# Tying weight splits behind copies, and one pass for bias and maximum, in a two-layer attention kernel

## The chip, the cores and the metric

One core of one Trainium2 chip runs the whole program. The metric is device time in microseconds, the median of three runs: 751.36 us before the change (750.59 to 751.94). A profile of one execution stands beside it, with the start and end of each instruction on each engine: TensorE (PE in the profile, PEld for its weight loads), VectorE (DVE), ScalarE (ACT), GpSimd (POOL) and SyncE (SP, which issues nearly all DMAs).

## The reference

Two layers on 256 positions of width 1024, 16 heads of 64. Layer 0 mixes three dilated windows of attention with rotary positions, layer 1 is a forgetting attention; each is followed by a SwiGLU block of width 2816, and a last RMS norm ends the program. All arrays are float32. The part of layer 1 that the change touches:

```
s = jnp.einsum('bihd,bjhd->bhij', qi, k).astype(jnp.float32) * scale
s = s + ci[..., None] - ck[:, :, None, :]
s = jnp.where(key_pos[None, :] <= qpos[:, None], s, NEG_INF)
p = jax.nn.softmax(s, axis=-1)
return jnp.einsum('bhij,bjhd->bihd', p, vf)
```

Here `c` is the running sum of the log forget gates. In layer 0 the queries and keys get `partial_rotary` first, a product with cosines plus a permuted product with sines.

## The kernel before, in words

**Split products.** TensorE multiplies in a reduced form of fp32. To keep precision each float32 operand is split into a high half (`wh` for weights; ACT copies the raw tile, L74) and a low half (`wl`; DVE subtracts the high half from the raw tile, L78), and each product is three matmuls (`mm3`, L197 and L202): high by high, high by low, low by high. So each weight tile that arrives costs ACT and DVE an instruction for each 1024 columns; `split` issues them.

**The stream of weights.** `order` lists all weight pieces in the order in which they are used. `weights(name, i)` loads and splits everything up to two pieces ahead (`AHEAD = 2`) and returns the piece wanted. A piece comes as two DMAs of 512 KB into `raw` (five buffers), and each is split into `wh` and `wl` (four buffers each). A raw buffer is free again when the low half has read it. The program is written in one stream; a scheduler orders each engine's instructions by what is written first, except that `first()` moves an instruction up to 300 places ahead, and `issue_after(x)` holds one back until x has been issued. Each engine then works strictly in its order.

**Layer 0.** The projections run unit by unit (one of queries, keys or values of one group for a quarter of the heads, 48 matmuls of 256 columns for a query or key unit). `rotated` turns a query or key unit: a shuffle (L433), a product with the cosines straight from PSUM (`read`, L434), a product with the sines (L435) and an addition (L436). A projection's PSUM tile (`mm`, two buffers) is free again after L433 and L434. For the first unit, `rcos` and `rsin` are first multiplied by the rows' norm factors (L569).

**Layer 1.** Heads go in four quarters of four heads; a quarter is a query unit, a key unit and, for the last quarter, a value unit. `proj_feat` gives queries or keys in PSUM, and ACT copies them to `fb` (L939). After the first half of the next unit PE computes the scores of the quarter's first pair of heads (`scores_b`, L855), and after its second half those of the second pair. For each pair of heads:

- DVE adds the bias, 384 columns for each head, from PSUM and `bias` to `p` (L861);
- DVE takes the negated maximum of 128 and of 256 columns (L865), two query blocks of each head;
- ACT takes the exponential with that maximum as bias and sums the row (`exps`, L283);
- DVE takes the reciprocal of the sums (L870), and ACT (L872) and DVE (L873) scale.

Then `trans_b` transposes the four heads' probabilities on PE (L293, from `p` to PSUM), copies them to `pt` (L297), and `pv_b` multiplies with the values (L304) and splits the result (`oth`, `otl`). The `bias` tile comes by a DMA issued on SP from a buffer in memory, and POOL adds the causal mask to two of its blocks (L841). Low halves of two weight calls are kept in the list `behind` and issued after the gates' scan or after the last bias addition (`release`).

Of the kernel before, what the change touches and what calls it, by code (L numbers as in the profile page):

```python
# [12 lines left out]
AF = mybir.ActivationFunctionType  # L13
# [18 lines left out]
def trunk(ctx: ExitStack, tc: tile.TileContext, T, out):  # L32
# [10 lines left out]
    def first():  # L43

        return tc.high_priority(offset=300)
# [22 lines left out]
    euler = cst.tile([P, 1], F32, name="euler")  # L68
    nc.gpsimd.memset(euler, math.e)

    def split(pair, view, src, early=True, after=None):
        hi, lo = pair
        with first() if early else nullcontext():
            a = nc.scalar.activation(view(hi), src, AF.Copy)  # L74

            def low(after=None):
                with tc.issue_after(after.ins) if after else nullcontext():
                    return nc.vector.tensor_tensor(view(lo), src, view(hi).bitcast(F32), op=ALU.subtract)  # L78

            if isinstance(after, list):  # L80
                return after.append(low)
            return a, low(after)


    def piece(key, todo=None):
        if key[0][:2] == "dn" and key[1] == LATE:
            wh, wl = (y.rearrange("p k c -> p (k c)") for y in fm_tile("ot", KT, 1))
        else:
            wh, wl = (wp.tile([P, WIDE], F32R, tag=y, name=y, bufs=4) for y in ("wh", "wl"))
        if key == GATED:  # L90
            wh, wl = (y.rearrange("p (k c) -> p k c", k=KT) for y in (wh, wl))
        for c in range(2):
            raw = wp.tile([P, 1024], F32, tag="raw", name="raw", bufs=5)
            u = slice(c * 1024, (c + 1) * 1024)
            nc.sync.dma_start(raw, T[key[0]][key[1]][:, u])
            view = lambda y, u=u: y[:, u]
            if key == GATED:
                raw = raw.rearrange("p (k c) -> p k c", c=256)
                view = lambda y, c=c: y[:, c * 4:c * 4 + 4, :256]
            cut = lambda after=None, raw=raw, view=view: split((wh, wl), view, raw, False, after)  # L100
            if todo is None:
                cut()
            else:
                todo.append(cut)
        if key == GATED:
            cut = lambda after=None: split((wh, wl), lambda y: y[:, :, 256:], wf32, False, after)
            todo.append(cut)
        return wh, wl

# [35 lines left out]
    ready = {}  # L145
    state = {"next": 0}

    def weights(nm, i, after=None, ahead=AHEAD):

        upto = order.index((nm, i)) + ahead  # L150
        while state["next"] <= min(upto, len(order) - 1):
            key = order[state["next"]]
            cuts = []
            ready[key] = piece(key, cuts)
            for cut in cuts:
                cut(after)
            state["next"] += 1
        return ready.pop((nm, i))

# [365 lines left out]
    def later(i, fn, *a):  # L525
        due.setdefault(i, []).append((fn, a))

    quads = [{"hq": hq, "fm": {}, "pt": {}, "v": {}} for hq in range(4)]
    for i, (hq, g, w) in enumerate(a_units):
        quad = quads[hq]  # L530
        if i == 3:
            o = o_next
        elif i:

            wt = weights("a_in", hq * 9 + g * 3 + w, read if i > 4 else None)
        if i != 3 and (w < 2 or g == 0 and hq > 1):
            o = psum("mm")
        if i == 1:
            ident = const("ident", [P, P])
            rcos = const("rcos", [P, S])  # L540
            rsin = const("rsin", [P, S])
        if i == 2:
            mask0 = const("mask0", [P, 3 * P])
            mask12 = const("mask12", [P, S])
        if i in (24, 31):
            x.append(hrow("x"))
            t = len(x) - 1
            nc.sync.dma_start(x[t], T["x"][t * P:(t + 1) * P, :])
        if w < 2:
            for c in range(2):  # L550
                if i == 3 and c == 0:
                    continue
                proj_feat(xt, wt, o[:, c * S:(c + 1) * S], c, (KT // 2, rstd_a) if i == 2 and c == 1 else None)
            if i == 2:
                values_12(quad["v"], lead)

                wt = weights("a_in", 1)
                o_next = psum("mm")
                rb = psum("tr")

                def rows():
                    for t in range(2):
                        nc.tensor.matmul(rb[:, t * P:(t + 1) * P], r_a[t].to_broadcast([P, P]), ident,
                                         start=True, stop=True)

                proj_feat(xt, wt, o_next[:, :S], 0, (6, rows))
                with first():
                    for c in (rcos, rsin):
                        nc.vector.tensor_tensor(c, c, rb[:, :S], op=ALU.mult)  # L569
            q, read = rotated(o, g, w)  # L570
            quad["fm"][g, w] = q
            if w == 1:

                j = i + (hq == 0)
                if g == 0:
                    for pr in range(2):
                        later(j + 2 + pr, scores_a, quad, g, pr)
                else:
                    later(j + 3 - g, scores_a, quad, g)
                if g == 2:  # L580
                    later(j + 1, softmax_a, quad)
                    j = 9 * hq + 11 + 2 * (hq == 0)
                    for pr in range(2):
                        later(j + pr, trans_a, quad, pr)
                        later(j + 1 + pr, pv_a, quad, pr)
        elif g == 0 and hq > 1:
            for t in range(2):
                proj_tok(xt, wt, o[:, t * S:(t + 1) * S], t)
            quad["v"][0] = v_tile(o, r_a)
        elif i > 1:  # L590


            half = hq % 2 if g == 0 else g - 1
            if half == 0:

                lead = [psum("mm" if g else "o") for _ in range(2)]
            proj_pair(xt, wt, lead, half)
            if half and g == 0:
                vs = [v_tile() for _ in range(2)]
                for t in range(2):  # L600
                    v_pair(vs, lead[t], t, r_a[t])
                for y in range(2):
                    quads[hq - 1 + y]["v"][0] = vs[y]
            elif half:
                values_12(quad["v"], lead)
        for fn, a in due.pop(i, ()):
            fn(*a)
# [239 lines left out]
    def scores_b(hq, pr):  # L847
        b = bq[hq]
        nm = stat_tile("nm_b", 4)
        den = stat_tile("den_b", 4)  # L850
        pt = b.setdefault("pt", {})
        scs = [psum("sc") for _ in range(2)]
        for qb in range(2):
            for h in range(2):
                last = nc.tensor.matmul(scs[h][:, qb * P:qb * P + (qb + 1) * P], b[0][own[h], pr, qb * P:(qb + 1) * P],  # L855
                                        b[1][own[h], pr, :(qb + 1) * P], start=True, stop=True)
        for h in range(2):
            s = p_tile()
            with first():
                bias_h = b["bias", pr][:, h * 3 * P:(h + 1) * 3 * P]  # L860
                added = nc.vector.tensor_tensor(s[:, :3 * P], scs[h][:, :3 * P], bias_h, op=ALU.add)  # L861
            for qb in range(2):
                j = h * 2 + qb
                sv = s[:, qb * P:qb * P + (qb + 1) * P]
                nc.vector.tensor_reduce(nm[:, j:j + 1], sv, axis=AX.X, op=ALU.max, negate=True)  # L865
                exps(sv, nm, den, j)
            pt[pr, h] = s
        release(added)
        c = stat_tile("c_b", 4)
        nc.vector.reciprocal(c, den)  # L870
        for h in range(2):
            nc.scalar.activation(pt[pr, h][:, :P], pt[pr, h][:, :P], AF.Copy, scale=c[:, h * 2:h * 2 + 1])  # L872
            nc.vector.tensor_scalar(pt[pr, h][:, P:3 * P], pt[pr, h][:, P:3 * P], c[:, h * 2 + 1:h * 2 + 2], None,  # L873
                                    op0=ALU.mult)
        return last
# [43 lines left out]
    for hq in range(2):  # L919
        for pr in range(2):  # L920
            later(3 + 2 * hq, bias, hq, pr)
    for i, (hq, w) in enumerate(b_units):
        if i < 3:
            continue
        wt = weights("b_in", hq * 3 + w, behind if i in (3, 5) else None)
        o = psum("mm")
        if w < 2:
            for c in range(2):
# [7 lines left out]
                    fn(*a)  # L936
            bq[hq][w] = ap.tile([P, 2, S], F32, tag=f"fm{w}", name=f"fb{w}", bufs=2)
            with first():
                nc.scalar.activation(bq[hq][w], o.rearrange("p (a b) -> p a b", a=2), AF.Copy, scale=(0.125, 1.0)[w])  # L939
            if w == 1:  # L940
                j = i + 1

# [150 lines left out]
```

## Time and profile before

| | |
|---|---|
| median of three runs | 751.36 us |
| profiled execution | 752.26 us |
| its span, first to last instruction | 750.5 us |
| TensorE busy in the span | 740.2 us |
| DVE busy | 500.7 us |
| ACT busy | 373.7 us |
| POOL busy | 67.3 us |
| granted TensorE clock, mean | 0.997 |

The span and what lies around it (1.76 us) make up the profiled execution. Times in the rows of a timeline are microseconds from the span's start; a row has start, duration, engine, line, operation, what is written from what, shapes and a count; idle time of the engine before it stands in brackets with what ended it. In rows of groups the mean of one instruction is in nanoseconds. On DVE and ACT an instruction's record overlaps the next one's by some 0.07 to 0.1 us, so what an instruction occupies is read from start to start. Layer 0's attention ends near 260 us, the first SwiGLU block near 450, layer 1's attention runs to about 565, and the second SwiGLU block ends the program.

### The profile page before, as it was taken

The numbers are of one execution on the slowest core, as the hardware profiler recorded it, in microseconds if no ns is written. First come the engines' busy times: TensorE is split into PE (matmuls) and PEld (weight loads), VectorE is DVE, ScalarE is ACT, GpSimd is POOL, SyncE is SP. The second block draws the span as 40 slices with busy tenths as digits, with TensorE's granted clock in tenths as the row PEclk, the third lists the DMA queues.
The fourth block names the chain that finished last, engine by engine and source line by source line (L and its number), as shares of the span: only waits on it lengthen the run. The fifth ranks groups of instructions, "written<-read, shape, count | busy, mean of one in ns | idle before, by whom it ended". The sixth has DMA issues, their size and how long they took to land.

```text
span 750.5 us, 14329 instructions
## 1 busy us (share of the span) xinstructions
PE 740.2 (99%) x5916; PEld 680.1 (91%) x5916; DVE 500.7 (67%) x752; ACT 373.7 (50%) x617; POOL 67.3 (9%) x98
## 2 busy tenths in 40 slices
PE   9999999999999999999999999999999999999996
PEld 7998989999998789999999988989889999999995
DVE  6987978876879376554556365799867545456533
ACT  7635537437427365444445355467556444445521
POOL 0600004004004000000000004312000000000001
PEclk9999999999999999999999999999999999999998
DMA  9865544645646267656567543784537665656601
GB/s 332 302 195 170 169 142 156 210 142 169 198 133 200 88 225 242 204 179 205 181 198 250 169 129 127 268 252 155 166 95 235 217 205 179 199 193 213 210 1 56
DMA packets 39441, 138.07 MB, mean 184 GB/s; under 512 B 4528, under 2 KB 5840, under 8 KB 39376
## 3 DMA queue, kind: packets, MB, share of 16 engines
q1 hardware_dynamic: 39232, 137.01, 55.3%
q8 instruction: 46, 0.75, 0.4%
q14 instruction: 19, 0.16, 0.1%
q10 hardware_dynamic: 144, 0.15, 0.1%
HBM read 136.07 MB, written 1.07 MB: 183 GB/s over the span
## 4 chain that ended last, share of the span: by engine, by line
PE 93%; ACT 2%; DVE 2%; DMA 2%; issue 1%; SPq 0%; POOL 0%; POOLq 0%; DVEq 0%; ACTq 0%
PE ps_mm L202 32%; PE ps_mm L197 17%; PE ps_tr L202 9%; PE ps_sc L202 8%; PE ps_o L202 7%; PE ps_tr L197 5%; PE ps_sc L197 4%; PE ps_o L197 4%; PE ps_o L304 2%; PE ps_tr L293 1%; DMA otl<-in_lead 1%; PE ps_sc L450 1%; PE ps_sc L466 1%; PE ps_sc L855 1%; ACT wh L74 1%; DMA raw<-in_a_in 1%
## 5 line engine op out<-in xcount | busy, mean ns | idle before, releaser
L74 ACT ACTIVATE wh<-raw 128x1024 fp32r<-128x1024 f32 x236 | 243.0, 1054 | 247.5 <-PE ps_mm L202 85.8
L78 DVE TENSOR_TENSOR wl<-raw,wh 128x1024 fp32r<-128x1024 f32 x236 | 287.7, 1238 | 81.8 <-ACT wh L74 81.5
L197 PE MATMUL ps_mm<-xt,wh 128*128 128x256 f32 x816 | 228.2, 280 | 0.7 <-DVE qk L434 0.7
L202 PE MATMUL ps_mm<-xt,wl 128*128 128x256 f32 x816 | 226.3, 277 | 0.1
L202 PE MATMUL ps_mm<-xt,wh 128*128 128x256 f32 x816 | 226.2, 277 | 0.0
L197 PEld LDWEIGHTS ps_mm<-xt,wh 128*128 128x128 f32 x816 | 153.3, 188 | 4.4 <-issue 3.3
L202 PEld LDWEIGHTS ps_mm<-xt,wl 128*128 128x128 f32 x816 | 153.4, 188 | 0.5 <-DVE wl L78 0.5
L202 PEld LDWEIGHTS ps_mm<-xt,wh 128*128 128x128 f32 x816 | 153.7, 188 | 0.0
L202 PE MATMUL ps_tr<-xt,wl 128*128 128x256 f32 x304 | 83.9, 276 | 0.0
L202 PE MATMUL ps_tr<-xt,wh 128*128 128x256 f32 x304 | 83.9, 276 | 0.0
L197 PE MATMUL ps_tr<-xt,wh 128*128 128x256 f32 x304 | 83.7, 276 | 0.0
L692 DVE TENSOR_TENSOR sa<-ps_tr,sa 128x256 f32<-128x256 f32 x38 | 16.1, 424 | 74.1 <-PE ps_tr L202 74.0
L202 PEld LDWEIGHTS ps_tr<-xt,wl 128*128 128x128 f32 x304 | 57.1, 188 | 0.0
L202 PEld LDWEIGHTS ps_tr<-xt,wh 128*128 128x128 f32 x304 | 57.1, 188 | 0.0
L197 PEld LDWEIGHTS ps_tr<-xt,wh 128*128 128x128 f32 x304 | 56.9, 188 | 0.0
L279 POOL COPY v<-v 32x256 f32<-32x256 f32 x64 | 36.1, 563 | 180.3 <-ACT v L275 177.6
L197 PE MATMUL ps_mm<-wh,xt 128*128 128x512 f32 (+1 forms) x144 | 50.1, 348 | 0.0
L202 PE MATMUL ps_mm<-wl,xt 128*128 128x512 f32 (+1 forms) x149 | 49.3, 336 | 0.0
L202 PE MATMUL ps_mm<-wh,xt 128*128 128x512 f32 (+1 forms) x149 | 49.2, 335 | 0.0
L167 POOL TENSOR_SCALAR rs<-ssq 128x1 f32<-128x1 f32 x7 | 2.1, 307 | 425.2 <-ACT junk L176 425.2
L197 PE MATMUL ps_sc<-wh,ah 128*128 128x512 f32 x80 | 31.4, 392 | 0.0
L202 PE MATMUL ps_sc<-wl,ah 128*128 128x512 f32 (+1 forms) x82 | 31.3, 385 | 0.0
(224 smaller groups left out, 1112.9 us busy)
## 6 DMA issues: line engine op xcount, KB each, us to landing
raw<-in_gu SPq DMA_DIRECT2D x88, 512.0 KB, 4.8
raw<-in_a_in SPq DMA_DIRECT2D x68, 512.0 KB, 4.4
raw<-in_dn SPq DMA_DIRECT2D x44, 512.0 KB, 4.5
raw<-in_b_in SPq DMA_DIRECT2D x24, 512.0 KB, 5.0
raw<-in_a_out SPq DMA_DIRECT2D x8, 512.0 KB, 4.5
raw<-in_b_out SPq DMA_DIRECT2D x8, 512.0 KB, 4.9
bias<-sums SPq DMA_DIRECT2D x8, 384.0 KB, 6.3
grow<-in_norms SPq DMA_DIRECT2D x4, 512.0 KB, 5.4
```

Of the source, the lines that this page charges most:

```text
L74: a = nc.scalar.activation(view(hi), src, AF.Copy)
L78: return nc.vector.tensor_tensor(view(lo), src, view(hi).bitcast(F32), op=ALU.subtract)
L167: nc.gpsimd.tensor_scalar(m, s, rest, None, op0=ALU.add)
L197: nc.tensor.matmul(o, sh, mh, start=start, stop=False)
L202: last = nc.tensor.matmul(o[:, u], s, m[:, u], start=False, stop=end and u.stop == n)
L279: nc.gpsimd.tensor_copy(v[1 + a % 2][n:n + 32, a // 2 * S:a // 2 * S + S], by_t[a * 32:a * 32 + 32, t, g])
L293: nc.tensor.transpose(tr[:, i * P:(i + 1) * P], b, ident)
L304: nc.tensor.matmul(o[h * HD:(h + 1) * HD], v[:, c:c + HD], w(h), start=start, stop=stop)
L450: nc.tensor.matmul(scs[h][:, qb * P:qb * P + (qb + 1) * P], q[hr[h], pr, qb * P:(qb + 1) * P], k[hr[h], pr, :(qb + 1) * P], start=True, st ...
L466: nc.tensor.matmul(sc[h][c, o:o + 64], q[hr[h], pq, qb * P + a * 32:qb * P + a * 32 + 32], k[hr[h], pq].rearrange("p (b n) -> p b n", b=2) ...
L692: nc.vector.tensor_tensor(a, u, sg, op=ALU.mult)
L855: last = nc.tensor.matmul(scs[h][:, qb * P:qb * P + (qb + 1) * P], b[0][own[h], pr, qb * P:(qb + 1) * P], b[1][own[h], pr, :(qb + 1) * P], ...
```

## The change

Four edits:

- In layer 1, `weights` is given the last copy of queries or keys to `fb` (`held`), and the high halves that it issues on ACT are held back until that copy has been issued.
- `scores_b` replaces the addition of 384 columns and the two maxima by one instruction for each query block, `tensor_tensor_reduce`. It adds scores and bias, multiplies by -1, writes that to `p`, and takes the minimum into `nm`, which is then the negated maximum. The exponential reads `p` with scale -1. On DVE this is an instruction and a second one that reads out the accumulator.
- `release` is called with the last of these in place of the last addition.
- In layer 0, one low half of the weights called for in unit 2 is no longer issued at once but after `read`, the first rotary product.

```diff
+    def behind_(ins):
+        return tc.issue_after(ins.ins) if ins else nullcontext()
-    def split(pair, view, src, early=True, after=None):
+    def split(pair, view, src, early=True, after=None, hold=None):
         hi, lo = pair
         with first() if early else nullcontext():
-            a = nc.scalar.activation(view(hi), src, AF.Copy)
+            with behind_(hold):
+                a = nc.scalar.activation(view(hi), src, AF.Copy)
...
             if i == 2:
                 values_12(quad["v"], lead)
-                wt = weights("a_in", 1)
+                second = []
+                wt = weights("a_in", 1, second)
+                second.pop(0)()
...
             q, read = rotated(o, g, w)
+            if i == 2:
+                second.pop()(read)
...
         for h in range(2):
             s = p_tile()
-            with first():
-                bias_h = b["bias", pr][:, h * 3 * P:(h + 1) * 3 * P]
-                added = nc.vector.tensor_tensor(s[:, :3 * P], scs[h][:, :3 * P], bias_h, op=ALU.add)
+            bias_h = b["bias", pr][:, h * 3 * P:(h + 1) * 3 * P]
             for qb in range(2):
-                j = h * 2 + qb
-                sv = s[:, qb * P:qb * P + (qb + 1) * P]
-                nc.vector.tensor_reduce(nm[:, j:j + 1], sv, axis=AX.X, op=ALU.max, negate=True)
-                exps(sv, nm, den, j)
+                j, u = h * 2 + qb, slice(qb * P, qb * P + (qb + 1) * P)
+                with first():
+                    added = nc.vector.tensor_tensor_reduce(s[:, u], scs[h][:, u], bias_h[:, u], -1.0, -NEG, ALU.add,
+                                                           ALU.min, nm[:, j:j + 1])
+                nc.scalar.activation(s[:, u], s[:, u], AF.Exp, bias=nm[:, j:j + 1], scale=-1.0,
+                                     accum_out=den[:, j:j + 1])
...
+    held = None
     for i, (hq, w) in enumerate(b_units):
         if i < 3:
             continue
-        wt = weights("b_in", hq * 3 + w, behind if i in (3, 5) else None)
+        wt = weights("b_in", hq * 3 + w, behind if i in (3, 5) else None, hold=held)
...
             with first():
-                nc.scalar.activation(bq[hq][w], o.rearrange("p (a b) -> p a b", a=2), AF.Copy, scale=(0.125, 1.0)[w])
+                held = nc.scalar.activation(bq[hq][w], o.rearrange("p (a b) -> p a b", a=2), AF.Copy,
+                                            scale=(0.125, 1.0)[w])
```

PE and POOL keep their order of instructions. DVE, ACT and SP change, at these places.

DVE at the first rotary operation of layer 0, before (line numbers of the kernel before):

```order
L433 STREAM_SHUFFLE rt<-ps_mm 128x512
L78 TENSOR_TENSOR wl<-raw,wh 128x1024
L569 TENSOR_TENSOR rcos<-rcos,ps_tr 128x256
L569 TENSOR_TENSOR rsin<-rsin,ps_tr 128x256
L434 TENSOR_TENSOR qk_352<-ps_mm,rcos 128x512
L435 TENSOR_TENSOR rt<-rt,rsin 128x512
L78 TENSOR_TENSOR wl<-raw,wh 128x1024
```

and in the changed kernel (its lines are 5 to 7 higher here):

```order
L438 STREAM_SHUFFLE rt<-ps_mm 128x512
L576 TENSOR_TENSOR rcos<-rcos,ps_tr 128x256
L576 TENSOR_TENSOR rsin<-rsin,ps_tr 128x256
L439 TENSOR_TENSOR qk_351<-ps_mm,rcos 128x512
L440 TENSOR_TENSOR rt<-rt,rsin 128x512
L83 TENSOR_TENSOR wl<-raw,wh 128x1024
```

The low half that stood behind the shuffle now comes after the two products, and each later low half here moves one place back.

ACT around the copy of the second quarter's keys (`fb_5626` before, `fb_5622` after; `p<-p,c_b` are the scalings of the first quarter's second pair), before:

```order
L283 ACTIVATE p,den_b<-p,nm_b 128x128
L283 ACTIVATE p,den_b<-p,nm_b 128x256
L74 ACTIVATE wh<-raw 128x1024
L872 ACTIVATE p<-p,c_b 128x128 x2
L74 ACTIVATE wh<-raw 128x1024
L939 ACTIVATE fb_5626<-ps_mm 128x512
L74 ACTIVATE wh<-raw 128x1024 x3
```

and in the changed kernel:

```order
L874 ACTIVATE p,den_b<-p,nm_b 128x128
L874 ACTIVATE p,den_b<-p,nm_b 128x256
L79 ACTIVATE wh<-raw 128x1024
L881 ACTIVATE p<-p,c_b 128x128 x2
L949 ACTIVATE fb_5622<-ps_mm 128x512
L79 ACTIVATE wh<-raw 128x1024 x2
```

One split that stood between the scalings and the copy now stands behind the copy.

DVE in the last quarter, between the copies of the third quarter's transposes and the last scalings, before:

```order
L297 COPY pt<-ps_o 128x512
L865 TENSOR_REDUCE nm_b<-p 128x1 x4
L870 RECIPROCAL c_b<-den_b 128x4
L873 TENSOR_SCALAR p<-p,c_b 128x256
L861 TENSOR_TENSOR p<-ps_sc,bias 128x384 x2
L873 TENSOR_SCALAR p<-p,c_b 128x256
L865 TENSOR_REDUCE nm_b<-p 128x1 x3
L78 TENSOR_TENSOR otl<-ps_o,oth 128x256
L865 TENSOR_REDUCE nm_b<-p 128x1
L78 TENSOR_TENSOR otl<-ps_o,oth 128x256
L78 TENSOR_TENSOR wl<-raw,wh 128x1024
L870 RECIPROCAL c_b<-den_b 128x4
```

and in the changed kernel, where ISA is the fused instruction (with `p` as output) and its readout (`nm_b` alone):

```order
L302 COPY pt<-ps_o 128x512
L879 RECIPROCAL c_b<-den_b 128x4
L83 TENSOR_TENSOR wl<-raw,wh 128x1024
L882 TENSOR_SCALAR p<-p,c_b 128x256 x2
L83 TENSOR_TENSOR wl<-raw,wh 128x1024
L872 ISA p,nm_b<-ps_sc,bias 128x128
L872 ISA nm_b 128x1
...
L872 ISA p,nm_b<-ps_sc,bias 128x256
L872 ISA nm_b 128x1
L83 TENSOR_TENSOR wl<-raw,wh 128x1024
L83 TENSOR_TENSOR otl<-ps_o,oth 128x256 x2
L83 TENSOR_TENSOR wl<-raw,wh 128x1024
L879 RECIPROCAL c_b<-den_b 128x4
```

Four low halves of weights stand in this stretch where there was one, and the fused instructions of the first pair have moved ahead of the copies.

More of the change, by code (lines that the diff above doesn't have):

```diff
@@ L99, in piece @@
                 view = lambda y, c=c: y[:, c * 4:c * 4 + 4, :256]
-            cut = lambda after=None, raw=raw, view=view: split((wh, wl), view, raw, False, after)
+            cut = lambda after=None, hold=None, raw=raw, view=view: split((wh, wl), view, raw, False, after, hold)
             if todo is None:
@@ L105, in piece @@
         if key == GATED:
-            cut = lambda after=None: split((wh, wl), lambda y: y[:, :, 256:], wf32, False, after)
+            cut = lambda after=None, hold=None: split((wh, wl), lambda y: y[:, :, 256:], wf32, False, after, hold)
             todo.append(cut)
@@ L146, in trunk, with weights @@
     state = {"next": 0}
-    def weights(nm, i, after=None, ahead=AHEAD):
+    def weights(nm, i, after=None, ahead=AHEAD, hold=None):
         upto = order.index((nm, i)) + ahead
@@ L155, in weights @@
             for cut in cuts:
-                cut(after)
+                cut(after, hold)
             state["next"] += 1
```

## The prediction

> **What bounds the kernel now.** I read the head of the page first, then what TensorE waited for, then the timelines around each wait.
>
> ```profile
> span 750.5 us, 14329 instructions
> PE 740.2 (99%) x5916; PEld 680.1 (91%) x5916; DVE 500.7 (67%) x752; ACT 373.7 (50%) x617; POOL 67.3 (9%) x98
> ```
>
> ```profile
> PE ps_sc L855 <- ACT fb L939: 1.6, 1, 1.6
> PE ps_o L313 <- DVE mhalf L65: 0.9, 1, 0.9
> PE ps_mm L197 <- DVE qk L434: 0.7, 1, 0.7
> ```
>
> TensorE (PE) is the bound: its order of instructions is the same in both kernels, so a change elsewhere only counts where PE stands still. Inside the work it stands still at two places: once for the copy of a key tile (`fb`, L939), once for a rotary product (`qk`, L434). The second row is the program's start and is not touched.
>
> Those rows give idle time after the modelled end of a matmul; what a stall costs is read from start to start.
>
> ```profile
> 484.74 0.28 PE L202 MATMUL ps_mm<-xt,wl 128*128 128x256 f32 x1
> 484.95 0.93 PE L855 MATMUL ps_sc<-fb,fb 64*128 64x128 f32 x8
> 491.25 0.28 PE L202 MATMUL ps_mm<-xt,wl 128*128 128x256 f32 x1
> 493.97 0.28 PE L202 MATMUL ps_mm<-xt,wl 128*128 128x256 f32 x1
> 495.88 0.93 PE L855 MATMUL ps_sc<-fb,fb 64*128 64x128 f32 x8 [1.63 <-ACT fb L939]
> ```
>
> Undisturbed, scores start 0.21 after the last projection matmul (484.74 to 484.95). Here it is 1.91 (493.97 to 495.88): the stall costs **1.70**. The scores could have started at 494.18. The key's own matmuls end near 491.5 (I read its last as the one at 491.25: 24 more at 0.11 lead to 494), so the copy had 2.6 us and was still late. Why, is in ScalarE's (ACT's) rows:
>
> ```profile
> 491.39 0.51 ACT L283 ACTIVATE p<-p,nm_b 128x256 f32<-128x256 f32 x1 [1.06 <-DVE nm_b L865]
> 491.90 0.39 ACT L283 ACTIVATE p<-p,nm_b 128x128 f32<-128x128 f32 x1
> 492.77 1.05 ACT L74 ACTIVATE wh<-raw 128x1024 fp32r<-128x1024 f32 x1
> 493.72 0.68 ACT L872 ACTIVATE p<-p,c_b 128x128 f32<-128x128 f32 x2
> 494.30 1.04 ACT L74 ACTIVATE wh<-raw 128x1024 fp32r<-128x1024 f32 x1
> 495.25 0.58 ACT L939 ACTIVATE fb<-ps_mm 128x512 f32<-128x512 f32 x1
> ```
>
> ACT works in order. Ahead of the copy stand four exponentials, of which the second waited for a maximum on VectorE (DVE), then a weight split, two scalings and a second weight split (494.30), which no one needs yet.
>
> The other stall, at the first rotary product:
>
> ```profile
> 26.37 0.74 DVE L433 STREAM_SHUFFLE rt<-ps_mm 128x512 f32<-128x512 f32 x1
> 27.32 1.33 DVE L78 TENSOR_TENSOR wl<-raw,wh 128x1024 fp32r<-128x1024 f32 x1 [0.21 <-ACT wh L74]
> 28.57 0.41 DVE L569 TENSOR_TENSOR rcos<-rcos,ps_tr 128x256 f32<-128x256 f32 x1
> 29.23 0.68 DVE L434 TENSOR_TENSOR qk<-ps_mm,rcos 128x512 f32<-128x512 f32 x1
> 28.96 0.28 PE L202 MATMUL ps_mm<-xt,wh 128*128 128x256 f32 x1
> 29.07 0.28 PE L202 MATMUL ps_mm<-xt,wl 128*128 128x256 f32 x1
> 30.05 0.36 PE L197 MATMUL ps_mm<-xt,wh 128*128 128x256 f32 x1 [0.71 <-DVE qk L434]
> ```
>
> The usual step is 0.11 (28.96 to 29.07); here it is 0.98, so the stall costs **0.87**. PE wants the PSUM bank that L434 reads.
>
> **The change part by part.** *The tied split at the start.* The low half at 27.32 goes behind L434. Without it L569 follows the shuffle, which hands over 0.07 before its end as its neighbours do, at 27.04; L434 is 0.66 behind L569 as before (28.57 to 29.23), so it runs from 27.70 to 28.4, and PE asks at 29.18. The whole 0.87 goes, with 0.8 to spare. The moved half runs near 29 instead, one place behind the second rotary operation; its weights belong to the unit after the next, 48 matmuls of 0.11 or 5 us further on, so PE does not miss it. It frees its staging buffer about 1.6 later, and on SP's queue one weight load moves behind the `grow` load; two units lie between that load and its use, which cover it. **Gain 0.87**, bounds 0.7 (the idle row) and 0.87.
>
> *Fused add and maximum.* Per pair of heads, two additions and four maxima on DVE become four fused instructions, each followed by a readout of its accumulator.
>
> ```profile
> L861 DVE TENSOR_TENSOR p<-ps_sc,bias 128x384 f32<-128x384 f32 x16 | 8.1, 545 | 4.2 <-PE ps_sc L855 4.2
> L865 DVE TENSOR_REDUCE nm_b<-p 128x1 f32<-128x256 f32 x16 | 6.5, 406 | 0.0
> L865 DVE TENSOR_REDUCE nm_b<-p 128x1 f32<-128x128 f32 x16 | 4.3, 270 | 0.0
> 744.57 0.43 DVE L987 SCALAR_TENSOR_TENSOR ps_sc<-hn 128x256 f32<-128x256 f32 x1
> 744.92 0.14 DVE L987 DVE_READ_ACCUMULATOR ps_sc<-hn 128x1 f32 x1
> 744.92 0.75 DVE L997 TENSOR_TENSOR xn<-hn,grow 128x256 f32<-128x256 f32 x2
> ```
>
> Today a pair costs 2 x 0.545 + 2 x 0.406 + 2 x 0.270 less about 0.07 of overlap at each of six, 2.0 us. The fused form is not in this trace. Its nearest row is L987, a two-input instruction with an accumulator: 256 elements occupy 0.35 (744.57 to 744.92), and the readout 0, since the next instruction starts with it. The 128 form then takes 0.35 less 128 elements, 0.136 by the two L865 rows: 0.21. A batch of four is 2 x (0.35 + 0.21) = 1.12 with free readouts, 1.7 if each costs its recorded 0.14. Upper end: half as much again as the six that it replaces, 3.2, or 0.8 for each. I take 1.12 plus 0.05 for each readout, 1.3. None of this is PE time; it shifts what DVE and ACT deliver.
>
> *Splits behind the copies.* Take the first quarter with DVE's rows:
>
> ```profile
> 482.18 1.02 DVE L861 TENSOR_TENSOR p<-ps_sc,bias 128x384 f32<-128x384 f32 x2 [4.19 <-PE ps_sc L855]
> 484.15 4.05 DVE L78 TENSOR_TENSOR wl<-raw,wh 128x1024 fp32r<-128x1024 f32 x2
> 489.31 1.72 DVE L873 TENSOR_SCALAR p<-p,c_b 128x256 f32<-128x256 f32 x2
> 489.32 1.29 POOL L841 TENSOR_TENSOR bias<-bias,causal 128x512 f32<-128x512 f32 x1 [2.21 <-DVE c_b L870]
> ```
>
> The two low halves end at 488.2 at the latest (484.15 + 4.05, and now they may start near 483.5). Reciprocal and two scalings follow at once, ahead of the POOL instruction at 489.32 that stretched them to 1.72, and end near 488.8; the second pair's four fused instructions end near 490.1, against 491.9 for today's last maximum. ACT: scalings to 488.9, split to 489.9, four exponentials of 0.44 (491.90 to 492.77 is two) to 491.6, split to 492.6, scalings to 493.2, and then the copy at once, done at 493.75. PE asks at 494.18. **Gain 1.70**, with 0.4 to spare; if the exponentials come no earlier and only the split at 494.30 leaves, the copy ends 0.95 earlier (494.30 to 495.25) and 0.75 of the stall stays. Bounds 0.95 and 1.70; I take 1.70, since both the fusion and the order move the copy forward.
>
> *What is late next.* The splits that were held back pile up on ACT and DVE in front of the last quarter.
>
> ```profile
> L78 DVE TENSOR_TENSOR wl<-raw,wh 128x1024 fp32r<-128x1024 f32 x236 | 287.7, 1238 | 81.8 <-ACT wh L74 81.5
> 526.41 0.59 ACT L939 ACTIVATE fb<-ps_mm 128x512 f32<-128x512 f32 x1
> 530.05 1.28 DVE L297 COPY pt<-ps_tr 128x512 f32<-128x512 f32 x2
> 538.76 0.62 DVE L873 TENSOR_SCALAR p<-p,c_b 128x256 f32<-128x256 f32 x2
> 527.64 0.93 PE L855 MATMUL ps_sc<-fb,fb 64*128 64x128 f32 x8
> 538.63 1.13 PE L293 MATMUL ps_tr<-ident,p 128*128 128x128 f32 x8
> ```
>
> PE transposes the last probabilities at 538.63, and from the seventh transpose on, 0.66 later, it needs what L873 scaled at 538.76: today this only just fits. Afterwards, with PE 2.57 earlier, the need is at 536.72. The chain that leads there: scores at 525.07 (527.64 less 2.57); the key's matmuls end 2.65 before scores can start (494.18 less 491.25 and 0.28), so the copy starts at 522.45, no longer behind a split, which let it start only at 526.41 before. Four splits of 0.95 follow it. DVE has the low halves of the first two done at 526.1 (1.238 by the L78 row, less 0.07 of overlap: 1.16 each), four fused instructions at 527.2, three copies (1.28 for two) at 529.05, a low half at 530.25, scalings at 530.85, a low half at 532.0, four fused at 533.1, a low half at 534.25, two `otl` of 256 elements at 534.9, a low half at 536.05, the reciprocal and the two scalings at 536.6 and 536.95. Four low halves stand between the three copies and the last scalings where there was one. So PE waits about 0.1 with free readouts, and 8 x 0.14 = 1.1 more if each readout costs its recorded time: bounds 0 and 1.3. With my 0.05 each it is **0.5 lost**. Every other move (the `bias` loads one place ahead on SP, `otl` one place later) ends before PE asks.
>
> **Sum** against the profiled execution, 752.26 with 1.76 outside the span: 752.26 - 0.87 - 1.70 + 0.5 = 750.19. The median of the runs, 751.36, lies 0.90 below that execution, so the forecast is **749.3**.
>
> **A rule against it.** The Trainium skill, in "Vector Engine (DVE) Microarchitecture Reference", section "Points that are easy to get wrong", says that two-source instructions of the accumulating shape run at half throughput when both sources are in SBUF and not bf16. The L987 row has two fp32 sources in SBUF, and its 256 elements took 0.43, where half rate needs over 0.53, so the trace disagrees. Here one source is PSUM besides.
>
> **The rivals.** *Readouts at full price*: the last quarter's wait is 1.3, and 752.26 - 2.57 + 1.3 - 0.90 = 750.1, within 0.2%. For it: the readout has a record of 0.14; against: the next instruction starts with it.
>
> *Half rate*: each fused instruction spends its elements' time twice, on average 0.2 more; eight in the last chain add 1.6 to the 0.5, so 752.26 - 2.57 + 2.1 - 0.90 = 750.9. Nothing in the rows speaks for it but that the form is new. This is what the skill's rule would give, were it to hold.
>
> *The copy is still late*, since four exponentials and a split stay ahead of it: 0.75 of the stall remains, 752.26 - 0.87 - 0.95 + 0.5 - 0.90 = 750.0.
>
> *Slower*: DVE becomes the bound of the second attention.
>
> ```profile
> 499.48:514.83 15.35, 15.35 (x136) 13.97 (x135) 15.31 (x30) 10.08 (x28) 3.80 (x2) 1.00 0.77 247
> ```
>
> In the second quarter DVE is already busy for 15.31 of 15.35. If a fused instruction with its readout costs x instead of 0.28 (a quarter of 1.12), the last chain alone is 8 (x - 0.28) later; from x = 0.59 on that and the 0.1 take all of the 2.57 gained. At x = 0.8 the last quarter loses 4.3, and the second, where a pair would cost 3.2 against 2.0, twice 1.2: 752.26 - 2.57 + 4.3 + 2.4 - 0.90 = 755.5. Against: 0.43 at L987.
>
> **How the numbers follow.** Forecast 0.57, readouts 0.15, copy still late 0.10, half rate 0.08, slower 0.10. A measurement of this kernel tells 0.2%, 1.5 us, from no change. The forecast lies 2.1 below and is faster; the three in the middle, 0.33, lie within; the last is slower. The forecast's own range is 748.6 to 749.9. Nothing lost in the last quarter gives 748.8, and the runs of before lie up to 0.8 from their median, so the range begins at 748.4; it ends at 751.3 to hold the three middle cases.
>
> **What would show it.** TensorE's waits: L197 for `qk` gone, the score matmul's wait for `fb` gone; a new wait of the L293 transposes for the scaled `p` near 536.7, some tenths long. The fused rows near 0.30 and 0.43, next start 0.21 and 0.35 later. The prediction is wrong if the fused rows are over 0.5, if scores still wait for a copy, or if a wait over 1.5 stands in the last quarter.

## The result, and the profile after

The changed kernel takes 748.55 us (median of 6 runs, 748.25 to 749.19) against 751.37 (6 runs beside it, 750.59 to 752.11): a ratio of 0.996, 95% interval 0.995 to 0.997. In a second series it took 749.10 (6 runs) against 751.61, ratio 0.9966 (0.9954 to 0.9978). So it is 2.5 to 2.8 us faster; 749.3, so 2.1 faster, was forecast. The profiled execution, the fastest of the six, took 748.25 with a span of 746.5.

The head of the page of the changed kernel:

```profile
span 746.5 us, 14344 instructions
...
PE 738.7 (99%) x5916; PEld 679.2 (91%) x5916; DVE 492.3 (66%) x768; ACT 374.5 (50%) x617; POOL 66.8 (9%) x98
```

What TensorE waited for in it, all that is listed:

```profile
PE ps_o L318 <- DVE mhalf L65: 0.9, 1, 0.9
```

Both stalls are gone and no new wait has come: the one row left is the program's start. DVE is busy for 8.4 us less (500.7 before).

The start, VectorE's timeline of the changed kernel (start, duration, engine, line, operation, tiles):

```profile
25.94 0.74 DVE L438 STREAM_SHUFFLE rt<-ps_mm 128x512 f32<-128x512 f32 x1
26.59 0.40 DVE L576 TENSOR_TENSOR rcos<-rcos,ps_tr 128x256 f32<-128x256 f32 x1
...
27.24 0.68 DVE L439 TENSOR_TENSOR qk<-ps_mm,rcos 128x512 f32<-128x512 f32 x1
27.84 0.71 DVE L440 TENSOR_TENSOR rt<-rt,rsin 128x512 f32<-128x512 f32 x1
28.48 1.41 DVE L83 TENSOR_TENSOR wl<-raw,wh 128x1024 fp32r<-128x1024 f32 x1
```

TensorE's timeline there, around the matmul that wants the bank:

```profile
28.67 0.28 PE L207 MATMUL ps_mm<-xt,wl 128*128 128x256 f32 x1
28.79 0.28 PE L202 MATMUL ps_mm<-xt,wh 128*128 128x256 f32 x1
```

No low half stands between the shuffle and the product any more; it comes at 28.48, one place behind the second rotary operation. Before, TensorE went on 0.82 after the product's start (29.23 to 30.05). That would be 28.06 here, and TensorE, which ran 0.4 us earlier already ahead of this place in this execution, asked at 28.79 and kept its step of 0.11: 0.7 to spare.

The second quarter's scores, ScalarE's timeline of the changed kernel:

```profile
489.35 1.05 ACT L79 ACTIVATE wh<-raw 128x1024 fp32r<-128x1024 f32 x1
490.30 0.68 ACT L881 ACTIVATE p<-p,c_b 128x128 f32<-128x128 f32 x2
490.88 0.58 ACT L949 ACTIVATE fb<-ps_mm 128x512 f32<-128x512 f32 x1
491.36 1.99 ACT L79 ACTIVATE wh<-raw 128x1024 fp32r<-128x1024 f32 x2
```

and TensorE's:

```profile
491.94 0.28 PE L207 MATMUL ps_mm<-xt,wl 128*128 128x256 f32 x1
492.14 0.93 PE L864 MATMUL ps_sc<-fb,fb 64*128 64x128 f32 x8
```

The copy is done at 491.46 and the scores start at 492.14, 0.20 after the last projection matmul: the whole 1.70 is gone, with 0.7 to spare. The splits run behind the copy.

The fused instruction, by its groups (count | busy time, mean ns | idle before):

```profile
L872 DVE CUSTOM_DVE_ANT_0 p<-ps_sc,bias 128x256 f32<-128x256 f32 x16 | 6.7, 418 | 0.0
L872 DVE CUSTOM_DVE_ANT_0 p<-ps_sc,bias 128x128 f32<-128x128 f32 x16 | 4.6, 285 | 5.4 <-PE ps_sc L864 4.2 <-issue 1.1
L872 DVE DVE_READ_ACCUMULATOR2_ANT nm_b<- 128x1 f32 x32 | 2.6, 82 | 0.0
```

and one batch of four on VectorE's timeline:

```profile
495.80 0.28 DVE L872 CUSTOM_DVE_ANT_0 p<-ps_sc,bias 128x128 f32<-128x128 f32 x1
496.01 0.08 DVE L872 DVE_READ_ACCUMULATOR2_ANT nm_b<- 128x1 f32 x1
496.01 0.41 DVE L872 CUSTOM_DVE_ANT_0 p<-ps_sc,bias 128x256 f32<-128x256 f32 x1
496.36 0.08 DVE L872 DVE_READ_ACCUMULATOR2_ANT nm_b<- 128x1 f32 x1
...
496.91 0.68 DVE L302 COPY pt<-ps_tr 128x512 f32<-128x512 f32 x1
```

From 495.80 to 496.91 a batch of four takes 1.11, and each readout starts together with the next instruction: it costs nothing.

The last quarter, VectorE's timeline of the changed kernel:

```profile
535.22 0.62 DVE L882 TENSOR_SCALAR p<-p,c_b 128x256 f32<-128x256 f32 x2
535.75 1.28 DVE L302 COPY pt<-ps_tr 128x512 f32<-128x512 f32 x2
```

and TensorE's:

```profile
535.06 1.16 PE L298 MATMUL ps_tr<-ident,p 128*128 128x128 f32 x8
536.05 0.60 PE L298 MATMUL ps_o<-ident,p 128*128 128x128 f32 x4
```

The eight transposes take 0.99 until the next instruction (535.06 to 536.05), as long as in the kernel before (538.63 to 539.62). Unhindered they take 0.87, as in the run below with the hold in one unit (535.62 to 536.49). So TensorE loses 0.12 there, and lost as much before the change: against the kernel before nothing was lost where 0.5 was forecast.

### The profile page after: what moved, and what is told of

The parts are those of the page before. It is cut to its first block, busy times and chain, and to the rows that moved or that the text cites. A ratio compares the mean times of both kernels' runs of the same rounds, so it can differ in the third digit from the quotient of the medians.

```text
span 746.5 us, 14344 instructions
## 1 busy us (share of the span) xinstructions
PE 738.7 (99%) x5916; PEld 679.2 (91%) x5916; DVE 492.3 (66%) x768; ACT 374.5 (50%) x617; POOL 66.8 (9%) x98
## 4 chain that ended last, share of the span: by engine, by line
PE 98%; DVE 1%; ACT 0%; POOL 0%; issue 0%; POOLq 0%; DVEq 0%; ACTq 0%
PE ps_mm L207 34%; PE ps_mm L202 18%; PE ps_tr L207 9%; PE ps_sc L207 8%; PE ps_o L207 7%; PE ps_tr L202 5%; PE ps_sc L202 4%; PE ps_o L202 4%; PE ps_o L309 2%; PE ps_sc L391 2%; PE ps_tr L298 1%; PE ps_sc L864 1%; PE ps_sc L455 1%; PE ps_sc L471 1%; PE ps_tr L195 1%; PE ps_o L298 1%
## 5 line engine op out<-in xcount | busy, mean ns | idle before, releaser
L701 DVE TENSOR_TENSOR sa<-ps_tr,sa 128x256 f32<-128x256 f32 x38 | 16.1, 424 | 74.1 <-PE ps_tr L207 74.1
```

Of the source, the lines that this page charges most:

```text
L701: nc.vector.tensor_tensor(a, u, sg, op=ALU.mult)
```

## The experiments

**The parts apart.** Four kernels on one chip, against 751.61 for the kernel before (29 runs).

*The tied split alone*, in the kernel before:

```diff
-                wt = weights("a_in", 1)
+                second = []
+                wt = weights("a_in", 1, second)
+                second.pop(0)()
...
             q, read = rotated(o, g, w)
+            if i == 2:
+                second.pop()(read)
```

> The kernel before with the tied split at the rotary product alone; the second attention stays as before. Theory (the step costs what the one stall costs): TensorE's 0.98 step before L434's reader becomes 0.11, the time falls by 0.87 us, from 751.4 to 750.5, and the score matmul's 1.9 us step at the key copy stays. Rival (the whole stretch from 25 to 47 us of the span becomes tighter, as the two traces already shown suggest, where TensorE lost 1.59 us on the kernel before): the time falls by about 1.6, to 749.8. If the start gave nothing at the end, it would stay at 751.4.

Measured: 750.46, ratio 0.9984 (0.9976 to 0.9993), so 1.15 less, with an interval of 0.5 to 1.8, which holds the theory's 0.87 and the rival's 1.6 alike. No wait for `qk` is listed. TensorE's rows in the second attention:

```profile
480.64 0.93 PE L859 MATMUL ps_sc<-fb,fb 64*128 64x128 f32 x8 [0.82 <-ACT fb L943]
...
494.68 0.93 PE L859 MATMUL ps_sc<-fb,fb 64*128 64x128 f32 x8 [0.86 <-ACT fb L943]
```

Two waits for a key copy, the first of them in the first quarter, where the kernel before had none. ScalarE shows why:

```profile
479.04 1.06 ACT L74 ACTIVATE wh<-raw 128x1024 fp32r<-128x1024 f32 x1 [3.56 <-DMA raw<-in_b_in]
480.01 0.58 ACT L943 ACTIVATE fb<-ps_mm 128x512 f32<-128x512 f32 x1
```

The copy of the first key stands behind a split that itself waits for its weights to land. The two waits add up to 1.68, as much as the single 1.6 of before: the time lost at the copies is the same, and half of it has moved forward. So this part is worth what it gains at the start.

*The hold alone*: `held` and `hold=held` as in the change, with addition and maximum in two passes and the start as before.

```diff
-        wt = weights("b_in", hq * 3 + w, behind if i in (3, 5) else None)
+        wt = weights("b_in", hq * 3 + w, behind if i in (3, 5) else None, hold=held)
```

> The kernel before with the high halves held behind the copies alone; addition and maximum stay two passes, and the start is as before. Theory (the order and the fused form need each other): scores of the second quarter start on time but for some 0.3 us, since the maxima still end 0.9 later than in the changed kernel; but each pair costs VectorE 0.9 more than in the changed kernel, the two pairs ahead of the last transposes 1.8, and the changed kernel has 0.57 to spare there (scalings end 535.84, need at 536.41), so a wait of about 1.2 us stands before the last transposes. Together the time falls by 0.2, to 751.2. Rival (the order alone does it): 1.70 fall away and nothing is lost, 749.7.

Measured: 751.32, ratio 0.9993 (0.9984 to 1.0001): no difference that can be told. Its waits:

```profile
PE ps_mm L202 <- DVE qk L439: 0.9, 1, 0.9
...
PE ps_o L298 <- ACT p L877: 0.6, 1, 0.6
PE ps_sc L860 <- ACT fb L945: 0.5, 1, 0.5
```

The scores are late by 0.5 still, and 0.6 are lost before the last transposes: at the copy the order alone gains about 1.1 and gives back 0.6 of it. TensorE's last transposes also came in another order here, since it is a scheduler that sets it. (The 0.57 to spare in the expectation was read against the matmul behind the transposes, at 536.41. The need is the seventh and eighth transpose, where nothing is to spare.)

*The fused form alone*:

```diff
-                added = nc.vector.tensor_tensor(s[:, :3 * P], scs[h][:, :3 * P], bias_h, op=ALU.add)
-                nc.vector.tensor_reduce(nm[:, j:j + 1], sv, axis=AX.X, op=ALU.max, negate=True)
+                    added = nc.vector.tensor_tensor_reduce(s[:, u], scs[h][:, u], bias_h[:, u], -1.0, -NEG, ALU.add,
+                                                           ALU.min, nm[:, j:j + 1])
...
```

> The kernel before with addition and maximum in one pass alone; order of the weight splits and the start as before. Theory (the copy stands behind two weight splits on ScalarE, which the fused form does not move): the score matmul still waits for the copy, and the time falls by at most 0.3, to 751.1 to 751.4. Rival (the copy was late because the maxima were): with the batch of four 0.9 shorter the copy comes 0.9 earlier, the step of 1.91 becomes about 1.0, and the time falls by 0.9, to 750.5.

Measured: 751.63, ratio 0.9994 (0.9984 to 1.0004): no difference that can be told, as the theory had it. TensorE's rows:

```profile
481.57 0.93 PE L855 MATMUL ps_sc<-fb,fb 64*128 64x128 f32 x8 [0.89 <-ACT fb L939]
...
495.08 0.93 PE L855 MATMUL ps_sc<-fb,fb 64*128 64x128 f32 x8 [0.42 <-ACT fb L939]
500.82 1.48 PE L855 MATMUL ps_sc<-fb,fb 64*128 64x128 f32 x8 [0.62 <-DVE nm_b L863]
```

The second quarter's wait did shrink, as the rival said (0.42 idle in place of 1.63), but 0.89 were lost at the first key copy, again behind a split that waited for a load, and 0.62 at the next scores, which waited for VectorE to read their bank. The lost time only changed its place. The expectation says that the order of the weight splits stays as before; it did not. The scheduler put one more split ahead of the second quarter's copy, so that two stand there behind the scalings where there was one, in ScalarE's timeline:

```profile
492.55 2.00 ACT L74 ACTIVATE wh<-raw 128x1024 fp32r<-128x1024 f32 x2
494.45 0.57 ACT L939 ACTIVATE fb<-ps_mm 128x512 f32<-128x512 f32 x1
```

One split takes 0.95 and the wait left was 0.42. What the fused form would give with ScalarE's order kept was not run.

*Both, without the tied split*: the changed kernel with the first diff of this section taken out.

> The changed kernel without the tied split at the start: holding and fusion together. Theory (the stall at the copy goes, nothing is lost in the last quarter): 1.70 less than before, 749.7; the start's step of 0.98 is back. Rival (some of the 2.8 us that the change gained does not come from these stalls): the time is 748.9 or less, or 750.2 if the last quarter does lose the 0.5 of the prediction.

Measured: 749.91, ratio 0.9975 (0.9964 to 0.9986): 1.70 less, the theory's number. Its one wait behind the program's start:

```profile
PE ps_mm L202 <- DVE qk L439: 0.8, 1, 0.8
```

So hold and fusion bring 0.3 and 0.0 alone, neither to be told from nothing, and 1.7 (1.1 to 2.7) together; with the 1.15 of the start the parts give 2.85, and the whole change gave 2.5 to 2.8.

**Is there room in the last quarter?** The forecast loss did not appear. Either there was room, or the chain just fitted. Six passes that multiply the last scaled halves by one make them late:

```diff
             nc.vector.tensor_scalar(pt[pr, h][:, P:3 * P], pt[pr, h][:, P:3 * P], c[:, h * 2 + 1:h * 2 + 2], None,
                                     op0=ALU.mult)
+            for _ in range(3 if (hq, pr) == (3, 1) else 0):
+                nc.vector.tensor_scalar(pt[pr, h][:, P:3 * P], pt[pr, h][:, P:3 * P], 1.0, None, op0=ALU.mult)
```

> The changed kernel, with the vector scalings of the very last pair of heads followed by three passes that multiply the same halves by one: six more instructions of 0.27 us each from start to start, and one copy of 0.60 us moved between them, so the scaled p of the last transposes is ready 2.2 us later (6 x 0.27 + 0.60). Theory (the last quarter just fits: nothing is to spare there and nothing is lost): a wait of about 2.2 us stands before the last transposes, and the time rises by 2.2, from 748.55 to 750.8. Rival (the forecast 0.5 did not appear because the quarter has room): with 0.5 or more to spare the time rises by 1.7 or less, to 750.2 at most.

Measured: 749.15, ratio 0.9968 (0.9956 to 0.9981), beside 749.10 for the changed kernel on the same chip: no loss at all. But this does not show room. TensorE's rows of these transposes, with what stands between them left out:

```profile
535.23 0.82 PE L298 MATMUL ps_tr<-ident,p 128*128 128x128 f32 x6
...
537.47 0.33 PE L298 MATMUL ps_tr<-ident,p 128*128 128x128 f32 x1
...
538.00 0.33 PE L298 MATMUL ps_tr<-ident,p 128*128 128x128 f32 x1
```

The eight transposes have become six and two stragglers: the scheduler knew of the passes and put projection matmuls in between, so the experiment moved two things. The next kernel adds a chain of order, each of the last transposes behind the one before and the output projection behind them, which leaves TensorE's and ScalarE's order exactly that of the changed kernel:

```diff
         for i, b in enumerate(blocks):
-            nc.tensor.transpose(tr[:, i * P:(i + 1) * P], b, ident)
+            with behind_(state.get("tr") if state.get("pin") else None):
+                state["tr"] = nc.tensor.transpose(tr[:, i * P:(i + 1) * P], b, ident)
...
```

> The same six passes as in the run called e5_late_last, but with the order of TensorE and of ScalarE kept exactly that of the changed kernel (each of the last transposes is queued behind the one before, and the output projection behind them), so that TensorE can't take other matmuls first. Theory (the last quarter just fits): TensorE waits 2.2 us before the last transposes (6 x 0.27 + 0.60), and the time is 2.2 above the changed kernel's 748.55 to 749.10, so 750.8 to 751.3. Rival (there are 0.5 us or more to spare): 1.7 above or less, 750.2 to 750.8 or less, with a wait of 1.7 or less in the profile.

Measured: 750.83, ratio 0.9991 (0.9982 to 1.0001), 1.7 to 2.3 above the changed kernel's two medians. Those are from other chips; against the kernel before on each chip the gain fell to 0.9, from 2.5 and 2.8, so 1.6 to 1.9 were lost. Its wait for the late halves, from TensorE's list of waits:

```profile
PE ps_tr L299 <- DVE p L889: 1.6, 2, 1.4
```

VectorE's timeline, the scalings and the last five of the added passes:

```profile
535.60 0.62 DVE L886 TENSOR_SCALAR p<-p,c_b 128x256 f32<-128x256 f32 x2
...
536.93 1.22 DVE L889 TENSOR_SCALAR p<-p 128x256 f32<-128x256 f32 x5
```

and TensorE's timeline:

```profile
535.44 0.82 PE L299 MATMUL ps_tr<-ident,p 128*128 128x128 f32 x6
537.68 0.33 PE L299 MATMUL ps_tr<-ident,p 128*128 128x128 f32 x1 [1.42 <-DVE p L889]
538.21 0.33 PE L299 MATMUL ps_tr<-ident,p 128*128 128x128 f32 x1 [0.20 <-DVE p L889]
538.37 0.60 PE L299 MATMUL ps_o<-ident,p 128*128 128x128 f32 x4
```

The first `ps_o` transpose comes 2.93 after the first of the eight (535.44 to 538.37) where it came 0.99 after it: 1.94 lost. The scaled halves were ready at 538.15 (536.93 + 1.22) in place of 536.22 (535.60 + 0.62), 1.93 later and not 2.2, since most of the added passes took 0.20 and not 0.27. The listed wait of 1.6 would also fit the rival, but it counts from the modelled end of a matmul; from start to start TensorE lost all of the 1.93. So every tenth by which VectorE is later there is lost: the last quarter just fits.

**Is there room at the start?**

The shuffle of the first rotary product runs three times (`extra` is 3 there and 1 elsewhere):

```diff
-            nc.vector.stream_shuffle(tmp, ov, [i ^ 8 if i < ROT else i for i in range(32)])
+            for _ in range(extra):
+                nc.vector.stream_shuffle(tmp, ov, [i ^ 8 if i < ROT else i for i in range(32)])
...
```

> The changed kernel, with the first rotary shuffle run three times instead of once: two more VectorE instructions of 0.65 us each from start to start stand ahead of the first rotary product, 1.3 in all. Theory (the product is ready 0.8 before TensorE asks): a wait of about 0.5 us comes back at 29 us, and the time rises by 0.5, to 749.05. Rival (no room there): it rises by 1.3, to 749.85. Second rival (a stall at this place also slows the stretch behind it): 0.5 and another 0.6, 749.65.

Measured: 749.89, ratio 0.9975 (0.9966 to 0.9985), 0.8 above the changed kernel on the same chip. VectorE's timeline:

```profile
25.77 0.74 DVE L439 STREAM_SHUFFLE rt<-ps_mm 128x512 f32<-128x512 f32 x1
...
27.34 0.74 DVE L439 STREAM_SHUFFLE rt<-ps_mm 128x512 f32<-128x512 f32 x1
...
28.63 0.68 DVE L440 TENSOR_TENSOR qk<-ps_mm,rcos 128x512 f32<-128x512 f32 x1
```

and TensorE's:

```profile
29.05 0.28 PE L207 MATMUL ps_mm<-xt,wl 128*128 128x256 f32 x1
29.46 0.36 PE L202 MATMUL ps_mm<-xt,wh 128*128 128x256 f32 x1
```

The two shuffles cost 1.57 (25.77 to 27.34), and TensorE stood still for 0.30 (a step of 0.41 in place of 0.11), so in this execution 1.27 were to spare, against 0.7 in the changed kernel's. The profile speaks for the theory, with room that differs by half a microsecond between executions. The time, 0.8 above, is too coarse to tell the first theory from its rivals by itself; what it has beyond the 0.30 is not explained. The profiled execution took 749.01, less than the median, so the others may have stood still for longer.

**How much of the hold is needed?** Held in one unit only, the one after the second quarter's key:

```diff
-        wt = weights("b_in", hq * 3 + w, behind if i in (3, 5) else None, hold=held)
+        wt = weights("b_in", hq * 3 + w, behind if i in (3, 5) else None,
+                     hold=held if i == 7 else None)
```

> The changed kernel, with the high halves held behind a copy in one unit alone, the one after the key of the second quarter. Theory A (the hold is worth something at the first quarter's key too, where the copy otherwise stands behind a split that waits for a weight load; two of the runs already shown lost 0.9 us there): the time rises by up to 0.9, to 749.0 to 749.4, and the profile, where the load is late, shows a wait of the first scores for the key copy. Theory B (one held unit carries all that the hold is worth): 748.55, with no wait of TensorE in the second attention.

Measured: 748.72, ratio 0.9963 (0.9951 to 0.9976), and no wait of TensorE behind the program's start: theory B. On the same chip the changed kernel has 749.10. That the first key's copy can be late is shown by the two profiles above; that the hold there saves time is not shown, since here the load came in time without it.

**The changed kernel again**, for the start's part:

> The changed kernel as it is, beside the others on the same chip. Theory (the start's part is the one stall): it stays 0.9 below the version that holds and fuses without the tied split at the start (749.91), so 748.6 to 749.0. Rival (the start's part is 1.4 or more): 748.5 or less. In its profile no wait of TensorE after 2 us of the span.

Measured: 749.10, with the start's wait as its only one. The version without the tied split (749.91) ran on another chip, whose kernel before has the same median of 751.61, so the difference is 0.8. In the first series the change gained 2.8, 1.1 more than that version's 1.7. With the 1.15 of the tied split alone the start's part lies between 0.8 and 1.15 by the medians, which do not settle more than that.

## Where the prediction was right, and the step that failed

- **What bounds the kernel**: right. TensorE's two stalls were what could be gained; with both gone its list of waits is empty but for the program's start, and its 5916 matmuls come in the same order in both traces.
- **The tied split, gain 0.87**: right in mechanism, and in size within what can be told. In the four profiles without it the wait for `qk` is 0.7 (before), 0.9, 0.4 and 0.8 long by the lists of waits; the times give 1.15 (0.5 to 1.8). The upper bound of 0.87 was one execution's value and too tight: this stall is not the same in every execution. It also put the stretch behind the stall at nothing, which the profiles make doubtful (see the two paces of TensorE in the last section). The 0.8 to spare was 0.7.
- **Splits behind the copies, gain 1.70**: right in mechanism and size: 1.7 in the steps of the profile (0.20 in place of 1.91) and 1.70 in the times of hold and fusion together, where the interval is 1.1 to 2.7 and so exact a match is luck. That "both the fusion and the order move the copy forward" is seen in the single parts, where the wait for it shrank from 1.63 to 0.5 and 0.42; in time they bring 0.3 and 0.0 alone. The forecast let the copy end 0.4 before the need; it ended 0.7 before it.
- **Fused add and maximum**: 1.12 with free readouts was the measured batch (1.11). The 0.05 added for each readout was wrong; it is 0 from start to start. The L987 row, whose readout starts together with the next instruction, had said so, and I charged a third of its recorded 0.14 against it.
- **What is late next, 0.5 lost**: this is the step that failed, by its size. The chain was right: in the changed kernel TensorE came to the last quarter's scores 1.0 earlier than forecast (524.07, not 525.07), and VectorE's rows keep the forecast's distance from it (the reciprocal at 535.01, not 536.05). With free readouts TensorE would wait 0.1 by it; it loses 0.12, which the kernel before lost too, and the run with the six passes shows that the last quarter has no room. The other 0.4 of the 0.5 was the charge of 0.05 for each of eight readouts, which cost nothing. The loss measured, against the kernel before, is 0.
- **The sum** without it: 752.26 - 0.87 - 1.70 - 0.90 = 748.8, between the two medians of 748.55 and 749.10. Both lie within the range from 748.4 to 751.3, near its low end. That it comes out so close is in part luck: the profiled executions differ by 4.0, and the stalls alone make 2.57.
- **Half rate**: 128 more elements cost the fused form 0.14 (0.21 to 0.35 from start to start), as they cost the maxima by the two L865 rows (0.136), and not twice that. The rule of the Trainium skill in "Vector Engine (DVE) Microarchitecture Reference", section "Points that are easy to get wrong", speaks of two sources in SBUF and here one is PSUM, so these rows do not test it; the L987 row, which does, disagreed.
- **The rivals**: readouts at full price falls with the fused rows, half rate too. The copy is not late. VectorE did not become the bound: its price for a fused instruction with its readout is 0.28, far from the 0.59 at which it was to decide; what happens beyond that was not tried.

## What to carry to other kernels

Two remedies for one late copy may be worth nothing apart: the order of the weight splits gave 0.3, the shorter VectorE pass 0.0, both 1.7. In one profile of each alone, waits had come up at other places, in part because the scheduler had reordered other instructions. Before adding a price for a readout or another small record, look whether the next instruction starts with it. Here it did, and the price was zero; the share of its record that was charged out of caution was the error. And where a scheduler sets the order, a probe that adds or takes away work must keep the order of the engine under test, or it measures the scheduler.

## What the runs showed that was not expected

*A copy behind a split that waits for a load.* In the profiles of the tied split alone and of the fused form alone, 0.8 to 0.9 us were lost at the first quarter's scores, where the kernel before lost nothing in its own profile: ScalarE works in order, and the split ahead of the copy stood 3.56 and 3.59 for its weights. In the kernel before it stood 2.54, and the same copy came just in time.

*TensorE shows two paces.* 48 steps of a stretch of matmuls of 256 columns, TensorE's timeline of the kernel before, first and last of 49 rows:

```profile
31.78 0.28 PE L202 MATMUL ps_mm<-xt,wl 128*128 128x256 f32 x1
...
37.43 0.28 PE L202 MATMUL ps_mm<-xt,wl 128*128 128x256 f32 x1
```

and of the kernel with hold and fusion without the tied split, whose instructions up to there are those of the kernel before (its rows start one matmul earlier in the order):

```profile
31.74 0.28 PE L207 MATMUL ps_mm<-xt,wh 128*128 128x256 f32 x1
...
37.18 0.28 PE L207 MATMUL ps_mm<-xt,wh 128*128 128x256 f32 x1
```

They took 5.65 in the one and 5.44 in the other, 0.118 and 0.113 a step, with nothing waited for, at a mean granted clock of 0.997 in both. Over the 142 steps from the matmul behind the stalled one to the last ahead of the first attention scores it makes 0.6 us: 16.7 in the kernel before (30.25 to 46.97) and 16.1 in the changed kernel (28.90 to 44.99). So two profiled executions can differ by more than their stalls (the spans of before and after differ by 4.0, the times by 2.5 to 2.8).

The eleven profiles have a pattern that bears on the start's part. Of the four kernels without the tied split, all of which stall at the rotary product, three took 16.7 for these steps and one 16.1. The seven with it all took 16.1. So the tied split may be worth another 0.6 in some executions, as the rival in its expectation said, and the forecast's 0.87 would then be too small. That the stall causes the slower pace is not shown: one kernel stalled and kept the quicker one. What sets the pace is open.
